# Turning eight gated heads on VectorE and through DRAM instead of on TensorE, in a one-core hybrid mixer block

## The chip, the cores and the metric

The kernel runs on 1 core of one Trainium2 chip. The metric is the device time of one execution in microseconds (us). Three runs of the kernel before gave 973.75 us as the median, 973.37 and 974.31 us as the ends.

## What is computed

One layer of a streaming encoder on 512 positions with 1024 channels. The input is normalised, projected once, and the columns are split among three mixers and three merge gates; the merged result is projected, a SwiGLU sub-layer and a gated per-layer embedding follow. The change touches the first mixer and its gate:

```python
hn = rms_norm(h, g_mix_pre)
proj = hn @ w_in
z_sgu, z_conv, z_pool, z_gate = jnp.split(proj, SPLITS, axis=-1)
u, v = jnp.split(gelu(z_sgu), 2, axis=-1)
v = layer_norm(v, g_v, b_v)
# 8 heads of 128 channels, 4 blocks of 128 positions
mixed = einsum('hij,bnjhc->bnihc', w_masked, v) + b_s        # mixes positions inside a block
br_a = (u * mixed) @ w_sgu_out
# causal depthwise convolution, width 31, then layer norm and silu: branch b
merged = gates[0] * br_a + gates[1] * br_b + gates[2] * br_c
```

## The kernel before, in words

The kernel works on the transpose: channels stand on the 128 partitions, the 512 positions along the free axis. Each matrix product is done three times in a reduced-width float type (`mm3`): high half times high half, high times low, low times high. So each 128x1024 block of weights is read from DRAM into a buffer `raw` (3 of them, queue of SyncE), copied to `hi` by ScalarE and subtracted to `lo` by VectorE (3 buffers each); a tile of 128 output channels is 24 matmuls with 512 columns. `Weights.get` takes the next block and starts loading so that two more are ahead. The load of a block waits for the `lo` of the block three before it; its `hi` waits until TensorE has left the `hi` of three tiles before.

The spatial gating unit needs the positions on the partitions. So `natural` computes `v` and then `u` with positions on the partitions: for each of two halves of 512 channels four weight blocks (`kk`), and for each the four position blocks, two position blocks before the yield with `behind` 0 and two after it. `mix_head(h)` splits the head's `v` into halves (`v_split`), multiplies it with the head's 128x128 position matrix (3 matmuls into `ps_mix`), and VectorE computes `gated = (ps_mix + b) * u`, 128 positions by 4 blocks of 128 channels. `turn_head(h)` brings the channels back to the partitions: four TensorE transposes of 128x128 into `ps_tr`, then a ScalarE copy (high) and a VectorE subtraction (low) into `sgu_T[h]`.

The heads are mixed and turned between other products: heads 0 to 3 are mixed during the last four weight blocks of `u` (dictionary `heads`), heads 4 to 7 after the gate tiles 0 to 2; heads 0 and 1 are turned during `u`, 2 to 7 after gate tiles 0 to 3. `SGU_LAG` is the number of gate tiles that come before the first branch tile: `for n in range(KT + SGU_LAG)` makes gate tile n (24 matmuls, `ps_gate`, sigmoid by ScalarE into `merged[:, n]`) and, from `n = SGU_LAG` on, branch tile `n - SGU_LAG` (24 matmuls over the eight `sgu_T`, `ps_br`), which VectorE multiplies into `merged`. Branch tile 0 takes the heads in order, so head 7 is needed last, by matmuls 22 to 24.

VectorE works off the depthwise convolution in the background: 8 groups of channels, for each one start instruction and 30 taps (`conv_tap`, `acc <- h_conv, vec, acc`), each tap reading what the one before wrote. `drain(n)` takes the next n entries of the list `background`; `TAPS = (4, 3, 5, 3, 5)` says how many after each product: `TAPS[2]` in the gate and branch tiles of the gating unit, `TAPS[3]` in the `z` tiles of the pooling branch, `TAPS[4]` in the pooling branch's gate and branch tiles. What is left is drained before the last of these; then the sum over the channels of the convolution goes to TensorE (`ps_stat`) for the layer norm.

The order of the instructions on each engine is made when the kernel is built, by a list scheduler with a timeline of its own: among the instructions that it holds for ready, the one written first in the program goes first. `order()` pins VectorE, ScalarE and TensorE instructions written inside it behind what was written before them on their engine; taps and `gated` are so pinned, the halves `lo`, `v_split` and `sgu` are not. DMAs go through the queue of SyncE (SP) in the order that the scheduler gives.

Of the kernel before, what the change touches and what calls it, by code (L numbers as in the profile page):

```python
# [7 lines left out]

F32 = mybir.dt.float32
F32R = mybir.dt.float32r  # L10
# [2 lines left out]
AF = mybir.ActivationFunctionType  # L13
ALU = mybir.AluOpType
PSUM = bass.MemoryType.PSUM

P = 128
T = 512
H = 256
D = 1024  # L20
KT = D // P
NB = T // P
WIDTH = 31
DFF = 2816
FT = DFF // P
# [17 lines left out]

N_WARM = 8

TAPS = (4, 3, 5, 3, 5)
TAPS_U = 4


# [42 lines left out]
def hybrid_block(  # L92
# [7 lines left out]
    nc = tc.nc  # L100
    order = InOrder(tc)
    dve, act_e = order.engine(nc.vector), order.engine(nc.scalar)
    pe_order = InOrder(tc)
    pe = pe_order.engine(order.engine(nc.tensor))

    const = ctx.enter_context(tc.tile_pool(name="const", bufs=1))
    stream = ctx.enter_context(tc.tile_pool(name="stream", bufs=3))
    wide = ctx.enter_context(tc.tile_pool(name="wide", bufs=2))
# [5 lines left out]
    def bank(name):  # L114
        return psum.tile([P, T], F32, tag="ps", name=name)

    def wide_tile(name):
        return wide.tile([P, KT, T], F32, tag="wide", name=name)

    def slot(tag, name, dt=F32R, shape=(2, T)):  # L120
        return act.tile([P, *shape], dt, tag=tag, name=name, bufs=6 if tag == "tm" else 8)

    def t2(name, n=T):
        return tmp.tile([P, n], F32, tag="t2", name=name)
# [4 lines left out]

    vec = const.tile([P, N_VEC + WIDTH * KT], F32, name="vec")  # L130
    x_all = wide_tile("x_all")
# [19 lines left out]
    def col(name, k):  # L151
        i = VECS.index(name) * KT + k
        return vec[:, i:i + 1]

    def tap(k, j):
        i = N_VEC + k * WIDTH + j
        return vec[:, i:i + 1]
# [7 lines left out]
    ps = psum.tile([P, T], F32, tag="pst", name="ps_warm", bufs=1)  # L165
    for n in N_WARM * (T,) + (H,):
        pe.matmul(ps[:, :n], lhsT=warm_up[:, :P], rhs=warm_up[:, :n], start=True, stop=True)
    ident = const.tile([P, P], F32, name="ident")
    make_identity(nc, ident)
    cnt_i = const.tile([P, WINDOWS[-1]], I32, name="cnt_i")  # L170
    nc.gpsimd.iota(cnt_i, pattern=[[1, WINDOWS[-1]]], base=1, channel_multiplier=0)
    rcnt = const.tile([P, WINDOWS[-1]], F32, name="rcnt")
# [4 lines left out]
    def split(hi, lo, src):  # L177
        act_e.copy(hi, src)
        dve.tensor_tensor(out=lo, in0=src, in1=hi, op=ALU.subtract)
# [142 lines left out]
    def add_mix(*blocks):  # L322
        for b in blocks:
            weights.add(w_mix[b])
# [3 lines left out]
    add_mix(*range(C_V, C_V + 8))  # L328
    weights.add(w_sgu, "tm")
    add_mix(*range(C_U, C_U + 8))  # L330
    SGU_LAG = 4
    for n in range(KT + SGU_LAG):
        if n < KT:
            add_mix(C_M + n)
        if n >= SGU_LAG:
            add_mix(S_SGU + n - SGU_LAG)
    for g in GROUPS:
# [121 lines left out]
    with order():  # L459
        (c0, c1), cut = first_cuts(0)  # L460
        hi, lo = (w[:, c0:c1] for w in first[0])
# [4 lines left out]
        hi, lo = (w[:, slice(*cut)] for w in first[0])  # L466
# [55 lines left out]
    for k in range(N_RAW, KT):  # L522
        pair = []
        for _ in range(2):
            ps = bank("ps_ag")
# [3 lines left out]
            pair.append(ps)  # L529
            drain(TAPS[0])  # L530
        glu(k, *pair)


    def natural(dst, evacuate, taps):


        for c in range(2):
            banks = [bank("ps_nat") for _ in range(NB)]
            for kk in range(4):
                hi, lo = weights.get()  # L540
                for b in range(NB):
                    if b == NB // 2:
                        yield c, kk, 0
# [12 lines left out]
                if kk == 3:  # L556
                    for b in range(NB):
                        evacuate(dst, b, c, banks[b])
                yield c, kk, 1

    def blocks_of(t):
        return t.rearrange("p a b -> p (a b)").rearrange("p (n c) -> p n c", n=NB)

    v_all = blocks_of(wide_tile("v_all"))
    v_stats = const.tile([P, NB, 2, 6], F32, name="v_stats")

    def v_gelu(dst, b, c, ps):
        cs = slice(c * T, (c + 1) * T)
        act_e.activation(out=dst[:, b, cs], in_=ps, func=AF.Gelu_apprx_tanh)
        dve.bn_stats(out=v_stats[:, b, c, :], in_=dst[:, b, cs])  # L570

    g_bc = slot("tm", "g_bc", F32, (D,))
    nc.sync.dma_start(out=g_bc, in_=gb_v[0:1, :].broadcast_to([P, D]))
    b_bc = slot("tm", "b_bc", F32, (D,))
    nc.sync.dma_start(out=b_bc, in_=gb_v[1:2, :].broadcast_to([P, D]))
    for _ in natural(v_all, v_gelu, TAPS[1]):
        pass
# [11 lines left out]
                                scalar2=v_y[:, b:b + 1], op0=ALU.subtract, op1=ALU.mult)  # L589

    def v_gain(b):
        dve.tensor_tensor(out=v_all[:, b], in0=v_all[:, b], in1=g_bc, op=ALU.mult)
        nc.gpsimd.tensor_tensor(out=v_all[:, b], in0=v_all[:, b], in1=b_bc, op=ALU.add)

    background[:0] = [lambda f=f, b=b: f(b) for b in range(NB) for f in (v_norm, v_gain)]

# [1 line left out]
    for w in (sg_hi, sg_lo):  # L598
        masked = w.rearrange("p (h i) -> p h i", h=KT)
        dve.memset(masked[64:128, :, 0:64].bitcast(F32), 0.0)  # L600
    u_all = blocks_of(wide_tile("u_all"))

    def u_gelu(dst, b, c, ps):
        act_e.activation(out=dst[:, b, c * T:(c + 1) * T], in_=ps, func=AF.Gelu_apprx_tanh)

    sgu_T = [None] * KT
    gated = [None] * KT

    def mix_head(h):
        cs = slice(h * P, (h + 1) * P)  # L610
        vs = slot("tm", "v_split", shape=(2, NB, P))
        split(vs[:, 0], vs[:, 1], v_all[:, :, cs])
        ps = bank("ps_mix")
        mm3(ps, sg_hi[:, cs], sg_lo[:, cs], vs[:, 0], vs[:, 1], True, True)
        gated[h] = t2("gated")
        with order():
            dve.scalar_tensor_tensor(
                out=gated[h].rearrange("p (n c) -> p n c", n=NB),
                in0=ps.rearrange("p (n c) -> p n c", n=NB),
                scalar=col("b_sgu_s", h), in1=u_all[:, :, cs], op0=ALU.add, op1=ALU.mult)  # L620

    def turn_head(h):
        pt = bank("ps_tr")
        for b in range(NB):
            bs = slice(b * P, (b + 1) * P)
            pe.transpose(out=pt[:, bs], in_=gated[h][:, bs], identity=ident)
        sgu_T[h] = slot("br", f"sgu{h}")
        split(sgu_T[h][:, 0], sgu_T[h][:, 1], pt)


    heads = {(1, 0): ((), (0,)), (1, 1): ((), (1,)), (2, 1): ((0,), (2,)),
             (3, 0): ((1,), ()), (3, 1): ((), (3,))}
    for c, kk, behind in natural(u_all, u_gelu, 0):
        pe_order.on = c == 1 or kk == 3
        turned, mixed = heads.get((kk, behind), ((), ())) if c == 1 else ((), ())
        for h in turned:
            turn_head(h)
        for h in mixed:
            mix_head(h)
        if behind:  # L640
            drain(TAPS_U)
# [3 lines left out]
    merged = wide_tile("merged")  # L645
# [17 lines left out]

    for n in range(KT + SGU_LAG):
        if n < KT:
            gate_tile(merged[:, n, :], TAPS[2])
        if n < SGU_LAG:
            for h in ((2,), (3, 4), (5,), (6, 7))[n]:
                turn_head(h)
            for h in ((4,), (5, 6), (7,), ())[n]:  # L670
                mix_head(h)
        else:
            i = n - SGU_LAG
            ps = branch_tile(sgu_T, TAPS[2])
            dve.tensor_tensor(out=merged[:, i, :], in0=ps, in1=merged[:, i, :], op=ALU.mult)


    z_all = wide_tile("z_all")
# [86 lines left out]
    for n in range(KT):  # L765
        ps = branch_tile(conv_T, 0)
        t = t2("br")
# [66 lines left out]
    with order():  # L834
# [6 lines left out]
        for i in range(N_HALF):  # L841
            n = KT - N_HALF + i
# [9 lines left out]
        for i in range(N_HALF):  # L852
            n = KT - N_HALF + i
# [79 lines left out]
    for n in range(KT - 2):  # L933
        ps = bank("ps_fo")
# [31 lines left out]
    with order():  # L966
        ps, ps_last = bank("ps_fo"), bank("ps_fo")
# [40 lines left out]
        for n in range(N_LAST, KT - 1):  # L1008
            ps = bank("ps_pg")
# [24 lines left out]
def _arrays(x, p, g_mix_pre, w_in, w_sgu_s, b_sgu_s, g_sgu_v, b_sgu_v, w_sgu_out, w_dw, b_dw,  # L1034
# [51 lines left out]
```

## Time and profile before

| | |
|---|---|
| median of three runs | 973.75 us |
| the profiled execution's own time | 974.28 us |
| its span, first to last instruction | 972.5 us |
| TensorE (PE) busy | 966.9 us, 99% |
| VectorE (DVE) busy | 673.3 us, 69% |
| ScalarE (ACT) busy | 349.9 us, 36% |
| GpSimd (POOL) busy | 70.9 us, 7% |
| granted TensorE clock | 1.0 |
| bytes read from HBM and written to it | 97.68 MB, 2.10 MB |

The profile is of one execution, 0.53 us above the median. The share of busy time is a mean over stages with different limits; the views that matter are the chain of work that ended last, the engines' busy time by stretch, and the timeline around the gating unit, from about 155 to 278 us of the span.

### The profile page before, as it was taken

The numbers are of one execution on the slowest core, as the hardware profiler recorded it, in microseconds if no ns is written. First come the engines' busy times: TensorE is split into PE (matmuls) and PEld (weight loads), VectorE is DVE, ScalarE is ACT, GpSimd is POOL, SyncE is SP. The second block draws the span as 40 slices with busy tenths as digits, with TensorE's granted clock in tenths as the row PEclk, the third lists the DMA queues.
The fourth block names the chain that finished last, engine by engine and source line by source line (L and its number), as shares of the span: only waits on it lengthen the run. The fifth ranks groups of instructions, "written<-read, shape, count | busy, mean of one in ns | idle before, by whom it ended". The sixth has DMA issues, their size and how long they took to land.

```text
span 972.5 us, 11143 instructions
## 1 busy us (share of the span) xinstructions
PE 966.9 (99%) x4429; PEld 804.4 (83%) x4429; DVE 673.3 (69%) x868; ACT 349.9 (36%) x467; POOL 70.9 (7%) x51
## 2 busy tenths in 40 slices
PE   9999999999999999999999999999999999999998
PEld 6888888888888888888888988888888888888887
DVE  6997789999988899987555787544444442223684
ACT  7622333432224432156425353323232322223451
POOL 0100004000013712130000000000000000000000
PEclk9999999999999999999999999999999999999999
DMA  8832331322322332232337203222322333334311
GB/s 291 197 109 87 110 107 66 108 87 87 109 85 78 98 108 87 94 123 87 109 97 263 74 26 105 87 97 98 99 97 89 104 82 99 99 100 144 109 66 65
DMA packets 30724, 102.72 MB, mean 106 GB/s; under 512 B 3536, under 2 KB 4048, under 8 KB 30672
## 3 DMA queue, kind: packets, MB, share of 16 engines
q1 hardware_dynamic: 29808, 99.75, 31.0%
q0 software_dynamic: 720, 2.23, 1.3%
q8 instruction: 34, 0.56, 0.2%
q14 instruction: 18, 0.15, 0.0%
q10 hardware_dynamic: 144, 0.04, 0.0%
HBM read 97.68 MB, written 2.10 MB: 103 GB/s over the span
## 4 chain that ended last, share of the span: by engine, by line
PE 99%; DMA 1%; SPq 0%; DVE 0%; ACT 0%; issue 0%; DVEq 0%
PE ps_f L79 25%; PE ps_gate L79 13%; PE ps_br L79 13%; PE ps_fo L79 12%; PE ps_nat L79 9%; PE ps_ag L79 6%; PE ps_o L79 5%; PE ps_pg L79 5%; PE ps_z L79 4%; PE ps_first L79 3%; PE ps_ple L79 1%; PE ps_pool L79 1%; DMA first_all<-in_w_first 1%; PE ps_mix L79 1%; PE ps_stat L79 0%; PE ps_tr L79 0%
## 5 line engine op out<-in xcount | busy, mean ns | idle before, releaser
L79 ACT CAST hi<-raw 128x1024 fp32r<-128x1024 f32 (+2 forms) x160 | 165.2, 1033 | 459.4 <-PE ps_br L79 82.5
L79 DVE TENSOR_TENSOR lo<-raw,hi 128x1024 fp32r<-128x1024 f32 (+2 forms) x158 | 206.9, 1310 | 110.0 <-ACT hi L79 109.7
L79 DVE SCALAR_TENSOR_TENSOR acc<-h_conv,vec,acc 128x511 f32<-128x511 f32 (+14 forms) x240 | 183.1, 763 | 5.0
L79 PE MATMUL ps_f<-hg,hi 128*128 128x512 f32 (+1 forms) x608 | 183.3, 383 | 0.0
L79 PEld LDWEIGHTS ps_f<-hg,hi 128*128 128x128 f32 x608 | 113.1, 188 | 22.4
L79 PE MATMUL ps_gate<-hn,hi 128*128 128x512 f32 x384 | 119.0, 389 | 0.0
L79 PE MATMUL ps_f<-hg,lo 128*128 128x512 f32 (+1 forms) x304 | 116.4, 383 | 0.0
L79 PE MATMUL ps_fo<-f,hi 128*128 128x512 f32 x352 | 108.3, 389 | 0.0
L79 PEld LDWEIGHTS ps_gate<-hn,hi 128*128 128x128 f32 x384 | 72.0, 188 | 15.1
L79 PE MATMUL ps_nat<-hi,hn 128*128 128x512 f32 x256 | 78.8, 389 | 0.0
L79 PEld LDWEIGHTS ps_fo<-f,hi 128*128 128x128 f32 x352 | 66.1, 188 | 13.7
L79 PE MATMUL ps_gate<-hn,lo 128*128 128x512 f32 x192 | 74.8, 389 | 0.0
L79 PE MATMUL ps_fo<-f,lo 128*128 128x512 f32 x176 | 68.5, 389 | 0.0
L79 PEld LDWEIGHTS ps_f<-hg,lo 128*128 128x128 f32 x304 | 57.1, 188 | 11.3
L79 DVE TENSOR_TENSOR f<-ps_f,h_inv 128x512 f32<-128x512 f32 x22 | 15.2, 690 | 59.3 <-PE ps_f L79 59.3
L79 PEld LDWEIGHTS ps_nat<-hi,hn 128*128 128x128 f32 x256 | 48.0, 188 | 9.9
L79 PE MATMUL ps_nat<-lo,hn 128*128 128x512 f32 x128 | 49.8, 389 | 0.0
L79 PE MATMUL ps_ag<-hn,hi 128*128 128x512 f32 x160 | 49.2, 389 | 0.0
L79 PEld LDWEIGHTS ps_gate<-hn,lo 128*128 128x128 f32 x192 | 36.0, 188 | 7.5
L79 DVE TENSOR_TENSOR silu<-ps_f,h_inv 128x512 f32<-128x512 f32 x22 | 15.2, 690 | 36.7 <-PE ps_f L79 36.6
L79 PE MATMUL ps_br<-pool,hi 128*128 128x512 f32 x128 | 39.6, 389 | 0.0
L79 PE MATMUL ps_br<-sgu,hi 128*128 128x512 f32 x128 | 39.4, 389 | 0.0
(223 smaller groups left out, 1490.6 us busy)
## 6 DMA issues: line engine op xcount, KB each, us to landing
raw<-in_w_mix SPq DMA_DIRECT2D x90, 512.0 KB, 3.2
raw<-in_w_ffn_in SPq DMA_DIRECT2D x44, 512.0 KB, 3.2
raw<-in_w_ffn_out SPq DMA_DIRECT2D x16, 448.0 KB, 3.3
raw<-in_w_ffn_out SPq DMA_DIRECT2D x8, 512.0 KB, 3.5
raw<-in_w_ple_gate SPq DMA_DIRECT2D x8, 512.0 KB, 3.9
x_all<-in_xT SPq DMA_DIRECT2D x8, 256.0 KB, 7.2
h_all<-in_xT SPq DMA_DIRECT2D x4, 512.0 KB, 5.4
out_dram<-pg SPq DMA_DIRECT2D x7, 256.0 KB, 2.0
```

The costliest lines, as they stand in the source:

```text
L79: inst = op(*args, **kw)
```

## The change

The gated head is no longer transposed by TensorE. VectorE transposes it in blocks of 32 by 32 (`dve.transpose`, right behind `gated`, both pinned). What then still has to move, whole blocks of 32 partitions, goes through DRAM: four writes of 32 partitions each (pieces of 128 elements, 512 bytes) into a DRAM tile `home` (8 of them), and one read of 128x512 back into the low half of `sgu_T[h]`. `split_head(h)` copies it to the high half (ScalarE) and subtracts (VectorE), now from SBUF instead of PSUM. So that a block of 32 columns is a block of 32 channels, `v` and `u` lie head by head, within a head by groups of 32 channels and then by position block; the positions of `sgu_T` and of the branch tiles stand in another order, and the multiplication into `merged` puts them back by its access pattern. The identity matrix goes. `SGU_LAG` is 5: branch tile 0 comes after gate tile 5, where it came after gate tile 4, and the heads are split after gate tiles 0 to 4. `TAPS[3]` is 4: one tap more after each of the 8 `z` tiles.

```diff
-TAPS = (4, 3, 5, 3, 5)
+TAPS = (4, 3, 5, 4, 5)
...
+    dram = ctx.enter_context(tc.tile_pool(name="dram", bufs=KT, space=bass.MemoryType.DRAM))
...
-    ident = const.tile([P, P], F32, name="ident")
-    make_identity(nc, ident)
...
-    SGU_LAG = 4
+    SGU_LAG = 5
...
     def blocks_of(t):
-        return t.rearrange("p a b -> p (a b)").rearrange("p (n c) -> p n c", n=NB)
+        return t.rearrange("p a b -> p (a b)").rearrange("p (g n a) -> p n g a", n=NB, a=Q)
+    def of_head(t, h):
+        return t[:, h]
+    def grouped(t):
+        return t.rearrange("p (g a) -> p g a", a=Q)
...
-        split(vs[:, 0], vs[:, 1], v_all[:, :, cs])
+        split(vs[:, 0], vs[:, 1], of_head(v_tile, h))
...
+        gated, corners = t2("gated"), t2("corners")
+        sgu_T[h] = slot("br", f"sgu{h}")
         with order():
+            dve.scalar_tensor_tensor(out=gated, in0=ps, scalar=col("b_sgu_s", h),
+                                     in1=of_head(u_tile, h), op0=ALU.add, op1=ALU.mult)
+            dve.transpose(out=corners, in_=gated)
+        home = dram.tile([P, T], F32, name="home")
+        for i in range(NQ):
+            nc.sync.dma_start(
+                out=home[:, i * P:(i + 1) * P].rearrange("(q a) f -> a q f", q=NQ),
+                in_=corners[i * Q:(i + 1) * Q].rearrange("a (q f) -> a q f", q=NQ))
+        nc.sync.dma_start(out=sgu_T[h][:, 1].bitcast(F32), in_=home)
 
-    def turn_head(h):
-        pt = bank("ps_tr")
-        for b in range(NB):
-            bs = slice(b * P, (b + 1) * P)
-            pe.transpose(out=pt[:, bs], in_=gated[h][:, bs], identity=ident)
-        sgu_T[h] = slot("br", f"sgu{h}")
-        split(sgu_T[h][:, 0], sgu_T[h][:, 1], pt)
+    def split_head(h):
+        hi, lo = sgu_T[h][:, 0], sgu_T[h][:, 1]
+        split(hi, lo, lo.bitcast(F32))
...
-            for h in ((2,), (3, 4), (5,), (6, 7))[n]:
-                turn_head(h)
-            for h in ((4,), (5, 6), (7,), ())[n]:
+            for h in ((2,), (3,), (4,), (5, 6), (7,))[n]:
+                split_head(h)
+            for h in ((4,), (5, 6), (7,), (), ())[n]:
                 mix_head(h)
...
-            dve.tensor_tensor(out=merged[:, i, :], in0=ps, in1=merged[:, i, :], op=ALU.mult)
+            gate = merged[:, i, :].rearrange("p (n i b) -> p i n b", n=NB, i=NQ)
+            dve.tensor_tensor(out=gate, in0=ps.rearrange("p (i n b) -> p i n b", n=NB, i=NQ),
+                              in1=gate, op=ALU.mult)
```

More of the change, by code (lines that the diff above doesn't have):

```diff
@@ L6 @@
 from concourse._compat import with_exitstack
-from concourse.masks import make_identity
 F32 = mybir.dt.float32
@@ L22 @@
 NB = T // P
+Q = 32
+NQ = P // Q
 WIDTH = 31
@@ L561, in blocks_of @@
     def blocks_of(t):
-        return t.rearrange("p a b -> p (a b)").rearrange("p (n c) -> p n c", n=NB)
-    v_all = blocks_of(wide_tile("v_all"))
+        return t.rearrange("p a b -> p (a b)").rearrange("p (g n a) -> p n g a", n=NB, a=Q)
[3 more added lines that the diff above has]
+        return t.rearrange("p (g a) -> p g a", a=Q)
+    v_tile = wide_tile("v_all")
+    v_all = blocks_of(v_tile)
     v_stats = const.tile([P, NB, 2, 6], F32, name="v_stats")
     def v_gelu(dst, b, c, ps):
-        cs = slice(c * T, (c + 1) * T)
-        act_e.activation(out=dst[:, b, cs], in_=ps, func=AF.Gelu_apprx_tanh)
-        dve.bn_stats(out=v_stats[:, b, c, :], in_=dst[:, b, cs])
+        v = dst[:, b, c * T // Q:(c + 1) * T // Q]
+        act_e.activation(out=v, in_=grouped(ps), func=AF.Gelu_apprx_tanh)
+        dve.bn_stats(out=v_stats[:, b, c, :], in_=v)
     g_bc = slot("tm", "g_bc", F32, (D,))
@@ L591, in v_gain @@
     def v_gain(b):
-        dve.tensor_tensor(out=v_all[:, b], in0=v_all[:, b], in1=g_bc, op=ALU.mult)
-        nc.gpsimd.tensor_tensor(out=v_all[:, b], in0=v_all[:, b], in1=b_bc, op=ALU.add)
+        dve.tensor_tensor(out=v_all[:, b], in0=v_all[:, b], in1=grouped(g_bc), op=ALU.mult)
+        nc.gpsimd.tensor_tensor(out=v_all[:, b], in0=v_all[:, b], in1=grouped(b_bc), op=ALU.add)
     background[:0] = [lambda f=f, b=b: f(b) for b in range(NB) for f in (v_norm, v_gain)]
@@ L600, in hybrid_block @@
         dve.memset(masked[64:128, :, 0:64].bitcast(F32), 0.0)
-    u_all = blocks_of(wide_tile("u_all"))
+    u_tile = wide_tile("u_all")
+    u_all = blocks_of(u_tile)
     def u_gelu(dst, b, c, ps):
-        act_e.activation(out=dst[:, b, c * T:(c + 1) * T], in_=ps, func=AF.Gelu_apprx_tanh)
+        act_e.activation(out=dst[:, b, c * T // Q:(c + 1) * T // Q], in_=grouped(ps),
+                         func=AF.Gelu_apprx_tanh)
     sgu_T = [None] * KT
-    gated = [None] * KT
     def mix_head(h):
         cs = slice(h * P, (h + 1) * P)
-        vs = slot("tm", "v_split", shape=(2, NB, P))
-        split(vs[:, 0], vs[:, 1], v_all[:, :, cs])
+        vs = slot("tm", "v_split")
+        split(vs[:, 0], vs[:, 1], of_head(v_tile, h))
         ps = bank("ps_mix")
         mm3(ps, sg_hi[:, cs], sg_lo[:, cs], vs[:, 0], vs[:, 1], True, True)
-        gated[h] = t2("gated")
+        gated, corners = t2("gated"), t2("corners")
+        sgu_T[h] = slot("br", f"sgu{h}")
         with order():
[L617 to L620, printed above, removed]
-    def turn_head(h):
-        pt = bank("ps_tr")
-        for b in range(NB):
-            bs = slice(b * P, (b + 1) * P)
-            pe.transpose(out=pt[:, bs], in_=gated[h][:, bs], identity=ident)
-        sgu_T[h] = slot("br", f"sgu{h}")
-        split(sgu_T[h][:, 0], sgu_T[h][:, 1], pt)
+            dve.scalar_tensor_tensor(out=gated, in0=ps, scalar=col("b_sgu_s", h),
[10 more added lines that the diff above has]
+        split(hi, lo, lo.bitcast(F32))
     heads = {(1, 0): ((), (0,)), (1, 1): ((), (1,)), (2, 1): ((0,), (2,)),
@@ L634, in hybrid_block @@
         pe_order.on = c == 1 or kk == 3
-        turned, mixed = heads.get((kk, behind), ((), ())) if c == 1 else ((), ())
-        for h in turned:
-            turn_head(h)
+        done, mixed = heads.get((kk, behind), ((), ())) if c == 1 else ((), ())
+        for h in done:
+            split_head(h)
         for h in mixed:
@@ L667, in hybrid_block @@
         if n < SGU_LAG:
-            for h in ((2,), (3, 4), (5,), (6, 7))[n]:
-                turn_head(h)
-            for h in ((4,), (5, 6), (7,), ())[n]:
+            for h in ((2,), (3,), (4,), (5, 6), (7,))[n]:
+                split_head(h)
+            for h in ((4,), (5, 6), (7,), (), ())[n]:
                 mix_head(h)
```

## The prediction

> **What bounds the kernel now.** I read the page first: the span, the busy shares, the chain.
>
> ```profile
> span 972.5 us, 11143 instructions
> PE 966.9 (99%) x4429; PEld 804.4 (83%) x4429; DVE 673.3 (69%) x868; ACT 349.9 (36%) x467; POOL 70.9 (7%) x51
> PEclk9999999999999999999999999999999999999999
> PE 99%; DMA 1%; SPq 0%; DVE 0%; ACT 0%; issue 0%; DVEq 0%
> ```
>
> TensorE is busy for 966.9 of 972.5 us at full granted clock and is 99% of the chain. No wait can be taken away: the time falls only by work that leaves TensorE, and rises by every wait that is put into it. Next, how close the other engines are, by three stretches: the gating unit, the `z` tiles, the pooling branch up to the convolution's sum.
>
> ```profile
> core 0: us, PE busy (x) PEld busy (x) DVE busy (x) ACT busy (x) POOL busy (x), PEclk, DMA share, GB/s
> 138.00:277.00 139.00, 139.00 (x630) 115.25 (x629) 135.88 (x174) 43.27 (x58) 16.25 (x7) 1.00 0.26 88
> 277.00:337.00 60.00, 60.00 (x266) 49.67 (x266) 49.18 (x57) 23.46 (x31) 24.82 (x18) 1.00 0.27 86
> 337.00:421.00 84.00, 84.00 (x372) 69.53 (x371) 82.65 (x96) 22.76 (x27) 21.29 (x14) 1.00 0.32 106
> ```
>
> The reader is to see that VectorE, 69% on average, is full where the heads are turned (135.88 of 139) and again from 337 us; only the `z` tiles leave it 10.8 us. ScalarE and the DMA engines have room everywhere.
>
> **What goes: 32 transposes.** The chain in order of time around them, with the shares by line of its window of 70 us (155 to 225):
>
> ```profile
> by line: PE ps_gate L79 41.6%; PE ps_nat L79 38.0%; PE ps_mix L79 7.9%; PE ps_br L79 7.8%; PE ps_tr L79 5.0%
> 168.53 2.72 PE ps_nat L79 x12
> 171.25 0.68 PE ps_mix L79 x3
> 177.38 0.44 PE ps_tr L79 x4
> 177.81 0.70 PE ps_mix L79 x3
> 178.52 2.75 PE ps_nat L79 x12
> 205.31 0.70 PE ps_mix L79 x3
> 211.49 0.87 PE ps_tr L79 x8
> 217.83 5.44 PE ps_br L79 x24
> 228.71 5.44 PE ps_br L79 x24
> ```
>
> The transposes are 5.0% of 70 us, 3.5 us (0.109 us each, 0.44 us a head). Behind them the next pieces are longer than the same pieces elsewhere: 0.70 against 0.68 for three matmuls, 2.75 against 2.72 for twelve, 0.05 us at each of six places, 0.25 us in all. TensorE gets back **3.75 us**; the identity was made off the chain and is worth nothing. The Trainium skill, "VectorE: DVE Perf Modes", section "The three transpose paths", gives 390 ns for a TensorE transpose of 128x128 (bf16); by that 32 of them would be 12.5 us and the time about 961.5 us. The trace differs: the chain has 3.5 us of them, so I give that outcome no chance.
>
> **What comes: VectorE.** The nearest rows by size are the other operations on 128x512:
>
> ```profile
> L79 DVE SCALAR_TENSOR_TENSOR gated<-ps_mix,vec,u_all x8: 741/744/746, 175.1 to 209.7; 128x512 f32<-128x512 f32 x8
> L79 DVE TENSOR_TENSOR sgu<-ps_tr,sgu x8: 677/682/689, 184.0 to 217.0; 128x512 fp32r<-128x512 f32 x8
> L79 ACT CAST sgu<-ps_tr x8: 576/582/601, 178.1 to 213.2; 128x512 fp32r<-128x512 f32 x8
> L79 DVE TENSOR_TENSOR v_split<-v_all,v_split x8: 678/682/689, 164.8 to 190.3; 128x512 fp32r<-128x512 f32 x8
> L79 ACT CAST v_split<-v_all x8: 607/620/625, 162.5 to 185.7; 128x512 fp32r<-128x512 f32 x8
> L79 DVE TENSOR_SCALAR acc<-h_conv,vec x4: 542/543/2196, 200.5 to 340.1; 128x512 f32<-128x512 f32 x4
> L79 DVE TENSOR_TENSOR lo<-raw,hi x25: 691/1219/2319, 163.0 to 297.3; 128x1024 fp32r<-128x1024 f32 x24, 128x512 fp32r<-128x512 f32 x1
> ```
>
> No block transpose stands in the trace. Its lower end is the one-input 0.54 us, its upper end the twice as large `lo` with 1.22 us (each element costing double); I take 0.70 us, between the 0.68 and 0.74 us of the same size. Eight are 5.6 us (4.3 to 9.8). The splits change source only: VectorE takes 0.682 us from PSUM (`sgu`) and from SBUF (`v_split`), ScalarE 0.58 and 0.62 us, so 0.3 us more on ScalarE, which is idle half of the time. The new layouts of `v`, `u` and `merged` keep every count of elements; runs of 32 I price at nothing, the cover being ScalarE's idle time, and on VectorE each 0.1 us on their 20-odd instructions would be 2 us of the same lag as the transposes'.
>
> **What comes: the way through DRAM,** eight times four writes and a read on the SP queue.
>
> ```profile
> L205 SPq DMA_DIRECT2D raw<-in_w_mix x23: 327/328/328, 164.2 to 298.5; - x23
> raw<-in_w_mix SPq DMA_DIRECT2D x90, 512.0 KB, 3.2
> out_dram<-pg SPq DMA_DIRECT2D x7, 256.0 KB, 2.0
> raw<-in_w_pool SPq DMA_DIRECT2D x4, 256.0 KB, 2.6
> SPq L205 <- DVE lo L79: 121.5, 24, 7.8
> ACT hi L79 <- PE ps_gate L79: 34.0, 8, 5.2
> ```
>
> One issue is 0.33 us, so a head is 1.6 us of SP's time and 13 us in all. A write of 64 KB I take at the 2.0 us of the store of 256 KB, the read at the 2.6 us of the load of the same 256 KB; a quicker trip gains nothing, since nothing waits for it then; the upper end is 3.2 us and an issue of 0.33 us more on each, if a 512 KB weight load goes ahead of it in the queue. Behind the waiting writes stand the weight loads. SP sits idle for 121.5 us from 160 to 290 until a buffer is free, and the `hi` casts then wait 34.0 us in 8 cases for TensorE to leave a buffer, none for a load: a load 4 us late is covered, and the wait for a head's writes (2 us plus 1.6 us of issue) is within that.
>
> **Where it can reach TensorE: head 7 in branch tile 0.** VectorE's timeline, kernel before:
>
> ```profile
> 190.28 0.69 DVE L79 TENSOR_TENSOR v_split<-v_all,v_split 128x512 fp32r<-128x512 f32 x1
> 209.74 0.75 DVE L79 SCALAR_TENSOR_TENSOR gated<-ps_mix,vec,u_all 128x512 f32<-128x512 f32 x1
> 211.66 3.08 DVE L79 SCALAR_TENSOR_TENSOR acc<-h_conv,vec,acc 128x506 f32<-128x506 f32 x4
> 216.44 1.28 DVE L79 TENSOR_TENSOR sgu<-ps_tr,sgu 128x512 fp32r<-128x512 f32 x2
> 220.61 1.22 DVE L79 TENSOR_TENSOR lo<-raw,hi 128x1024 fp32r<-128x1024 f32 x1
> ```
>
> `gated` of head 7 starts at 209.74, on an engine without idle time; seven transposes ahead of it make that 214.6, its end 215.4, its transpose's end 216.1. The fourth write is issued 1.0 us later and lands 2.0 us on, 219.1; the read lands at 221.7; ScalarE 222.3; VectorE finishes a tap (up to 0.77, 3.08 over 4) and subtracts (0.68): 223.0 to 223.8. Needed: branch tile 0 began at 217.83, now 5.44 later for the gate tile put ahead and 3.75 earlier, 219.5; head 7 comes 21 of 24 matmuls in, 224.3. That is 0.5 to 1.3 us in hand. The cover is that gate tile; without it all is 5.4 us late. Since the margin is smaller than the doubt on the round trip I charge **0.3 us** of wait (ends 0 and 2.6 us, one transfer behind a load, 3.5, less the middle of the margin, 0.9).
>
> **What is late next: the taps.** VectorE has 5.6 us more to do and TensorE passes 3.4 us sooner, so the taps fall 9.0 us behind. The small halves need not: at 190.28 the half of head 7's `v` went in between taps, long before its use after 205. The taps' reckoning comes at the convolution's sum:
>
> ```profile
> DVE lo L79 <- ACT hi L79: 5.4, 5, 2.0
> DVE pool L79 <- ACT pool L79: 3.3, 2, 2.9
> 418.36 1.78 DVE L79 TENSOR_TENSOR sum_half<-conv_sum,sum_half 128x512 fp32r<-128x512 f32 x1
> 420.79 0.39 PE L79 MATMUL ps_stat<-sum_half,mean_mat 128*128 128x512 f32 x1
> ```
>
> The sum is ready at 420.14 and TensorE takes it at 420.79, 0.65 us in hand. Ahead of it, in the `z` stretch, VectorE has 10.8 us without work, most of it waits that a late tap can fill (5.4 us for `hi`, 3.3 us for `pool`). `TAPS[3]` moves 8 taps, 6.2 us at 0.77, from the pooling branch to the `z` tiles: 9.0 and 6.2 less 10.8 leaves 4.4 us behind at 337, and the 6.2 us that are then missing turn that into 1.8 us ahead. I cost it at nothing; the `z` stretch is its cover.
>
> **The sum,** against the profiled execution: 974.28 - 3.75 + 0.3 = 970.8 us. That execution is 0.53 us above the median of the runs, so 970.3 us, 0.35% less. A measurement of this kernel tells about 0.2% (1.9 us) from no change.
>
> **The rivals.**
> 1. VectorE becomes the bound in the gating unit. If taps keep their place ahead of the weights' `lo`, the one that ended at 221.83 ends 5.6 us later, 227.4. Its tile began at 228.71, the matmul that takes it 0.45 later (two of 0.227), and all that 3.75 sooner is 225.4. TensorE waits 2.0 us: 972.5 us, 972.0 against the median. With 1.22 us a transpose the `lo` ends 9.8 us later, the wait is 6.2 us and the time 976.2 us. For it: 135.88 of 139. Against: the row at 190.28. Chance 0.25, nine tenths of it up to 975.0.
> 2. The round trip is slow, and the change is slower. Place: head 7 in branch tile 0. If the last write and the read each go behind a weight load, the trip is 7.1 us longer, TensorE waits 6.2 us (0.9 in hand), and the time is 974.28 - 3.75 + 6.2 less 0.53: 976.2 us. The trip of 4.6 us may grow by 0.9 before it costs anything, by 4.6 before the gain is gone, by 6.6 before it is measurably slower. For it: a weight load goes through the same queue in every tile. Against: the scheduler may let TensorE go on with gate tile 6. Chance 0.18. A harsher form is that short pieces slow the write: 512 bytes each, where the stores in the trace have whole rows. The same section of the Trainium skill warns that a plain DMA whose access pattern makes the transposition is 19 times slower than one through the transposing unit; by that the write would take 38 us and the time be near 1005 us. No run here shows such pieces; they are contiguous, and VectorE has done the transposition within them: chance 0.02.
> 3. The taps are not made up. If only half of the 10.8 us can be filled, 9.0 - 5.4 - 0.65 = 2.95 us of waiting at `ps_stat`: 973.0 us against the median, no change. Against: the waits in the `z` tiles are for `hi` and `pool`, which a tap can precede. Chance 0.08.
>
> **How the numbers follow.** The forecast has 0.47; its own range is 969.7 (no wait, and the spread of the runs) to 971.3 us (1.3 us of wait). Faster by over 0.2% is below 971.8 us: 0.47 and 0.08 of rival 1 (waits under 1.8 us), 0.55. No change: 0.14 of rival 1 and rival 3, 0.22. Slower: rival 2 with its harsher form, 0.20, and 0.03 of rival 1, 0.23. The range of 969.7 to 975.0 leaves out rival 2 and the worst of rival 1.
>
> **What would show it.** Right: no `ps_tr`; gate and branch tiles follow each other with matmuls every 0.227 us from 185 on; a block transpose of 0.6 to 0.8 us behind each `gated`; writes landing in about 2 us and reads in under 3; head 7's subtraction done before the 22nd matmul of branch tile 0; VectorE with less than 5 us idle from 277 to 337. Wrong: a gap on TensorE in branch tile 0 released by `sgu` (rival 2), by `lo` in several tiles (rival 1), or at `ps_stat` (rival 3); a transpose of 1.2 us; ScalarE waiting for a read while `hi` casts stand behind it.

## The result, and the profile after

The change made the kernel slower: 981.62 us as the median of four runs (979.13 to 982.34) against 974.0 us for the kernel before, a ratio of 1.0077 with an interval of 1.0064 to 1.0089. The forecast was 970.3 us. The profiled execution took 981.05 us. Of the experiments below, one run of e13 took 1631 us and one of the kernel before, beside e14, 1073 us, at granted clocks of 0.56 and 0.85; the times and ratios leave these two out. From the page of the profiled execution, the span, the busy shares, the granted clock and the chain that ended last:

```profile
span 979.1 us, 11157 instructions
PE 967.0 (99%) x4397; PEld 803.4 (82%) x4397; DVE 679.1 (69%) x876; ACT 349.0 (36%) x467; POOL 70.8 (7%) x49
PEclk9999999999998999999999999999999999999999
PE 79%; DVE 15%; issue 3%; DMA 2%; ACT 0%; SPq 0%; DVEq 0%; ACTq 0%
```

TensorE has 32 instructions fewer, and its busy time is still 967 us: some of its matmuls ran slower. The chain, 99% TensorE before, has left it for VectorE in 15% of the span, and one slice of forty shows a clock below full. By stretch of the kernel (the gating unit, the `z` tiles, the pooling branch; the columns are busy time and count of each engine, the granted clock and the share of the DMA engines):

```profile
138.00:273.00 135.00, 134.63 (x594) 111.19 (x593) 127.66 (x168) 41.89 (x57) 14.43 (x6) 1.00 0.38 119
273.00:333.00 60.00, 54.48 (x225) 44.15 (x224) 56.46 (x68) 18.49 (x25) 20.87 (x14) 0.94 0.26 85
333.00:425.00 92.00, 90.77 (x401) 74.58 (x400) 86.90 (x96) 26.39 (x32) 28.08 (x17) 1.00 0.29 98
```

The gating unit, where the change was made, lost almost nothing: TensorE is busy for 134.63 of 135 us. The loss is in the `z` tiles behind it, where TensorE stood for 5.5 of 60 us and ran at a mean clock of 0.94. What TensorE waited for from 150 to 430 us, and what VectorE waited for from 160 to 290 us (total, times, longest, in us):

```profile
PE ps_pool L80 <- ACT pl_hi L80: 5.5, 2, 3.1
PE ps_gate L80 <- DVE lo L80: 1.2, 1, 1.2
PE ps_br L80 <- DVE lo L80: 0.4, 1, 0.4
```

```profile
DVE sgu L80 <- ACT sgu L80: 5.9, 4, 2.2
```

The two waits are at the pool maps, the small products `ps_pool` over the moving windows that are made between the `z` tiles. VectorE, on the other hand, stood for 5.9 us in the gating unit before it could subtract a head.

**The first wait.** The timeline of VectorE, with TensorE's and GpSimd's rows at the same place:

```profile
287.55 1.18 POOL L705 COPY win<-z_all 128x2 f32<-128x2 f32 x1
288.60 3.07 DVE L80 SCALAR_TENSOR_TENSOR acc<-h_conv,vec,acc 128x505 f32<-128x505 f32 x4
292.19 2.28 DVE L80 SCALAR_TENSOR_TENSOR acc<-h_conv,vec,acc 128x501 f32<-128x501 f32 x3
294.39 1.21 DVE L80 SCALAR_TENSOR_TENSOR win<-win,z_all 128x1020 f32<-128x1020 f32 x1
297.58 0.73 PE L80 MATMUL ps_pool<-pl_hi,hi 128*128 128x512 f32 x2 [2.42 <-ACT pl_hi L80]
```

GpSimd's part of the window ended at 288.73. VectorE took its own part at 294.39, 5.66 us later, because seven taps and a `lo` stood ahead of it in VectorE's queue. Before, the same distance was 1.4 us (292.04 to 293.45). TensorE's last matmul ahead of the map began at 294.77 and the next could have begun 0.227 us later, so TensorE lost 2.58 us; the view's 2.42 counts from the modelled end of that matmul.

**The second wait,** on VectorE after and, in the second fence, before:

```profile
304.75 0.63 POOL L705 COPY win<-win 128x4 f32<-128x4 f32 x1
311.88 1.20 DVE L80 SCALAR_TENSOR_TENSOR win<-win,z_all 128x1016 f32<-128x1016 f32 x1
313.01 0.15 DVE L80 TENSOR_TENSOR win<-win,rcnt 128x8 f32<-128x8 f32 x1
313.08 0.71 DVE L80 SCALAR_TENSOR_TENSOR acc<-h_conv,vec,acc 128x487 f32<-128x487 f32 x1
313.72 1.21 DVE L80 TENSOR_TENSOR lo<-raw,hi 128x1024 fp32r<-128x1024 f32 x1
314.86 0.15 DVE L80 TENSOR_TENSOR win<-win,z_all 128x8 f32<-128x8 f32 x1
```

```profile
306.43 0.63 POOL L689 COPY win<-win 128x4 f32<-128x4 f32 x1
307.69 1.21 DVE L79 SCALAR_TENSOR_TENSOR win<-win,z_all 128x1016 f32<-128x1016 f32 x1
308.82 0.16 DVE L79 TENSOR_TENSOR win<-win,rcnt 128x8 f32<-128x8 f32 x1
309.01 0.17 DVE L79 TENSOR_TENSOR win<-win,z_all 128x8 f32<-128x8 f32 x1
```

Before, VectorE's three steps of the window begin 0.63 us behind GpSimd's part and follow each other. After, VectorE comes to the first step 6.50 us behind GpSimd's part (305.38 to 311.88), with taps, two `lo` and two `pool` ahead of it, and a tap and a `lo` stand between the second step and the third, 1.78 us. ScalarE's `pl_hi` and TensorE's map can only come behind the third; TensorE lost 3.26 us.

**The clock behind the waits.** The busy times of the 3.5 us from 299.0 on, a little after the first wait:

```profile
299.00:302.50 3.50, 3.50 (x11) 2.69 (x10) 3.46 (x3) 0.00 (x0) 3.38 (x3) 0.51 0.48 150
```

The granted clock is 0.51, and the matmuls follow each other every 0.427 us instead of 0.227. The clock record holds half speed for 3.4 us at 299.1 and again at 316.1. The Trainium skill, "TensorE: Matmul & The Clock Gate", "Why this matters for your kernels", advises against pauses of over about 3 us between bursts of matmuls, since one idle window brings the clock down to half. The trace is stricter: here 2.58 us were enough.

**The account,** by adding up what the distances between TensorE's matmuls exceed 0.227 us: first pool map 2.69 us and 1.59 us at half clock; second 3.63 and 1.50; branch tile 0, 0.64; a gate tile at 345.5, 1.50; another spot 0.11. That is 11.66 us put in. Taken out: 3.75 us of transposes, and 1.19 us in the first 13 us of the span, where TensorE starts on the input and the change does nothing (this part differs from run to run). The net is 6.7 us; the spans differ by 6.6 us.

### The profile page after: what moved, and what is told of

Read it like the earlier page. It is cut to its first block, busy times and chain, and to the rows that moved or that the text cites. A ratio compares the mean times of both kernels' runs of the same rounds, so it can differ in the third digit from the quotient of the medians.

```text
span 979.1 us, 11157 instructions
## 1 busy us (share of the span) xinstructions
PE 967.0 (99%) x4397; PEld 803.4 (82%) x4397; DVE 679.1 (69%) x876; ACT 349.0 (36%) x467; POOL 70.8 (7%) x49
## 4 chain that ended last, share of the span: by engine, by line
PE 79%; DVE 15%; issue 3%; DMA 2%; ACT 0%; SPq 0%; DVEq 0%; ACTq 0%
PE ps_f L80 25%; PE ps_fo L80 12%; PE ps_br L80 9%; PE ps_gate L80 8%; DVE acc L80 8%; PE ps_ag L80 6%; PE ps_o L80 5%; PE ps_pg L80 4%; PE ps_nat L80 4%; DVE lo L80 4%; PE ps_first L80 3%; PE ps_ple L80 1%; DMA sgu<-home 1%; DVE v_all L80 1%; DMA home<-corners 1%
## 5 line engine op out<-in xcount | busy, mean ns | idle before, releaser
L80 DVE SCALAR_TENSOR_TENSOR acc<-h_conv,vec,acc 128x509 f32<-128x509 f32 (+14 forms) x240 | 188.5, 790 | 4.3
L80 PE MATMUL ps_z<-hn,hi 128*128 128x512 f32 x128 | 41.6, 406 | 0.0
```

The lines of the kernel that those rows point to most:

```text
L80: inst = op(*args, **kw)
```

## The experiments

Three theories of where the time comes from. The first: the 8 taps moved by `TAPS[3]` overfill VectorE in the `z` tiles. The second: the way through DRAM makes VectorE, which works its queue in order, stand before a split, and what is late there is paid in the `z` tiles. The third: the 5.6 us of block transposes alone do it. All can hold in part, so each was taken out alone and with others. Each kernel was timed beside the kernel before on the same chip; ratios are against that. The kernel before gave 973.6 to 974.0 us in these comparisons, so a difference between the times of two experiments carries a doubt of some 0.4 us from that alone.

**e1_taps3: the change without the moved taps**

```diff
-TAPS = (4, 3, 5, 4, 5)
+TAPS = (4, 3, 5, 3, 5)
```

> The changed kernel with TAPS[3] back at 3, so 8 taps (6 us of VectorE) leave the z tiles. In the changed kernel TensorE waits 2.6 and 3.3 us at two pool maps in the z tiles, and its clock is halved for 3.4 us after each. Theory A (VectorE has too much work: eight transposes of 0.70 us and 8 taps more ahead of the pool windows): the second wait shrinks by most of 4 us and the first by about 2, so both waits and one or both of the slow stretches go, 972 to 975 us. Theory B (VectorE lost 5.9 us standing at head 7 and others for the way through DRAM, and stays late): those 5.9 us are still lost before the z tiles, the waits shrink by 1 to 3 us, 976 to 979 us. Theory C (the taps alone): 970.5 us.

976.41 us, ratio 1.0025 (1.0015 to 1.0036). Of the 7.6 us, 5.2 go. TensorE's and VectorE's main waits:

```profile
PE ps_pool L80 <- ACT pl_hi L80: 2.6, 2, 2.4
DVE sgu L80 <- ACT sgu L80: 6.8, 4, 2.5
```

The first pool map still waits, with half clock for 3.4 us behind it, and VectorE's standing before the heads is there in full. The taps are the larger part and not all. Two more waits, at branch tile 0, are for a `lo` (0.8 us) and, this time, for a `hi` of ScalarE (0.3 us).

**e2_before_taps4: the moved taps alone, in the kernel before**

```diff
-TAPS = (4, 3, 5, 3, 5)
+TAPS = (4, 3, 5, 4, 5)
```

> The kernel before with TAPS[3] = 4 alone. Theory C (the taps alone make the waits at the pool maps): 978 to 982 us. Theories A and B (the z tiles have 10.8 us free on VectorE in the kernel before, so 6.2 us fit): 974 us, no change within 1.5 us.

975.04 us, ratio 1.0015 (1.0005 to 1.0024). TensorE's only wait behind the loading of the input is in a gate tile of the pooling branch, none is at a pool map:

```profile
PE ps_gate L79 <- DVE lo L79: 1.3, 1, 1.3
```

The same 8 taps cost 1.5 us here (975.04 against 973.59 us for the kernel before in this comparison) and 5.2 us in the changed kernel. They cost little by themselves; they cost more where VectorE comes late into the `z` tiles, or where its queue is woven otherwise.

**e3_no_dram: the change without the way through DRAM.** The split reads the block-transposed head directly, without writes and read.

```diff
-        home = dram.tile([P, T], F32, name="home")
-        for i in range(NQ):
-            nc.sync.dma_start(out=home[...], in_=corners[...])
-        nc.sync.dma_start(out=sgu_T[h][:, 1].bitcast(F32), in_=home)
+        turned[h] = corners
...
-        split(hi, lo, lo.bitcast(F32))
+        split(hi, lo, turned[h])
```

> The changed kernel without the way through DRAM: the split reads what VectorE transposed (32 by 32 blocks are left in the wrong places, so the output is not the reference's); no write, no read, everything else the same. Theory B (VectorE's 5.9 us of standing still for the reads): VectorE has no such wait, is up to 5.9 us earlier at the pool maps, and the time is 970 to 974 us. Theory A (work): VectorE is as late at the z tiles as its work makes it, 977 to 981 us.

974.35 us, ratio 1.0007 (0.9998 to 1.0016); against the change, 7.3 us less. The waits of TensorE and of VectorE:

```profile
PE ps_pool L80 <- ACT pl_hi L80: 2.8, 1, 2.8
DVE sgu L80 <- ACT sgu L80: 0.7, 1, 0.7
```

VectorE stands before the heads for 0.7 us instead of 5.9. One pool map, the second, still waits, with 6.8 us of half clock behind it. That execution is the slowest of ten, with 976.21 us. The mean granted clock of the ten goes with their times: 1.0 in the four of 972.77 to 973.54 us, 0.998 in four from 974.26 to 975.88 us, 0.996 in two (975.95 us and the profiled one). So the half clock doesn't come in every execution of the same kernel, and it makes up to 3 us of difference. The DMA way has a large part in the loss although no wait of TensorE names it.

**e4_before_turn: the block transposes alone, in the kernel before**

```diff
+            dve.transpose(out=t2("corners"), in_=gated[h])
```

Its result isn't used; the heads are turned by TensorE as before.

> The kernel before, TensorE transposing, with a block transpose of each gated head on VectorE besides, whose result nobody reads: 5.6 us of VectorE's work and nothing else of the change. Theory A: VectorE is 5.6 us later at the z tiles, the first pool map has about 2 us in hand and the second 1, so TensorE waits 2 to 4 us there and loses a slow stretch or two: 977 to 980 us. Theory B: the free time in the z tiles takes it, 974 to 975 us.

974.34 us, ratio 1.0007 (0.9997 to 1.0016): no change. The one wait is of 0.4 us:

```profile
PE ps_mix L79 <- DVE gated L79: 0.4, 1, 0.4
```

So 5.6 us more on a VectorE that is busy for 135.88 of 139 us cost nothing measurable in the kernel before: its taps move on (157 are begun when the `z` tiles begin, where it was 161), into time that is free later. The third theory, taken alone, falls.

**e7_no_dram_taps3: both taken away** (e3 with `TAPS[3]` at 3)

```diff
-TAPS = (4, 3, 5, 4, 5)
+TAPS = (4, 3, 5, 3, 5)
```

> The changed kernel with both: no way through DRAM (the split reads the blocks where VectorE left them, so the output is not the reference's) and TAPS[3] = 3. Theory AB (VectorE's lateness is a sum of its waits for the reads, the taps moved and the transposes, and TensorE stalls only beyond 2 to 3 us of it): no wait of TensorE at the pool maps, no slow clock, the 3.75 us of the transposes come back whole: 969.5 to 970.5 us. Theory D (the layouts or the shorter TensorE path alone make it late): a wait and a slow stretch stay, 973 us or more.

970.77 us, ratio 0.9970 (0.9959 to 0.9981). No pool map waits; what is left is the wait that the third rival spoke of:

```profile
PE ps_stat L80 <- DVE sum_half L80: 0.6, 1, 0.6
```

With three taps per `z` tile, the way through DRAM costs 976.41 - 970.77 = 5.6 us; with four, 7.3 us.

**e10_no_turn: e3 without the block transposes as well,** four taps. The split reads the gated head itself.

```diff
-        gated, corners = t2("gated"), t2("corners")
+        gated = t2("gated")
...
-            dve.transpose(out=corners, in_=gated)
-        turned[h] = corners
+        turned[h] = gated
```

> e3_no_dram (TAPS[3] = 4, no DRAM) also without VectorE's block transposes: the split reads the gated head as it is (output not the reference's). 5.6 us less of VectorE's work. Theory A (the transposes' 5.6 us take part in the lateness): the 3.0 us wait of e3_no_dram at the second pool map goes, 970 to 971 us. If the 8 taps moved are enough alone beside a TensorE that is 3.75 us earlier: the wait stays, 973 to 975 us.

971.61 us, ratio 0.9978 (0.9969 to 0.9987). TensorE's wait is that of e2, and no pool map waits:

```profile
PE ps_gate L80 <- DVE lo L80: 1.2, 1, 1.2
```

The transposes, worth nothing in e4, are worth 2.7 us here (974.35 - 971.61), beside the fourth tap; against the four runs of e3 with full clock (973.41 us in the middle) it is 1.8 us. The loads on VectorE don't simply add up: the transposes alone (e4, e7) or the moved taps alone (e2, e10) make no pool map late; transposes with taps (e3) or with standing before the heads (e1) do, and then the clock can drop.

**e8_late: the way through DRAM kept, the splits put behind their data.** Three taps; no split during `u`; the splits one gate tile later (head 6 two) and pinned, on ScalarE as on VectorE, behind what is written ahead of them; branch tile 0 after gate tile 6. These were changed together, and which of them does it was not separated.

```diff
-TAPS = (4, 3, 5, 4, 5)
+TAPS = (4, 3, 5, 3, 5)
...
-    SGU_LAG = 5
+    SGU_LAG = 6
...
-        split(hi, lo, lo.bitcast(F32))
+        with order():
+            split(hi, lo, lo.bitcast(F32))
...
-    heads = {(1, 0): ((), (0,)), (1, 1): ((), (1,)), (2, 1): ((0,), (2,)),
-             (3, 0): ((1,), ()), (3, 1): ((), (3,))}
+    heads = {(1, 0): ((), (0,)), (1, 1): ((), (1,)), (2, 1): ((), (2,)),
+             (3, 1): ((), (3,))}
...
-            for h in ((2,), (3,), (4,), (5, 6), (7,))[n]:
+            for h in ((0, 1), (2,), (3,), (4,), (5,), (6, 7))[n]:
```

> The changed kernel with the way through DRAM, TAPS[3] = 3, and the splits later and pinned in program order: heads 0 and 1 after gate tile 0, 2 to 5 after gate tiles 1 to 4, 6 and 7 after gate tile 5, branch tile 0 after gate tile 6 (SGU_LAG = 6). The work is that of e1_taps3. Theory B (the place of the subtraction in VectorE's queue, ahead of its data, is what costs): VectorE waits under 1.5 us for the reads instead of 6.8, TensorE does not wait at the pool maps: 969.5 to 971.5 us. Theory A (work): as e1_taps3, 975 to 977 us.

971.78 us (971.63 to 972.54), ratio 0.9981 (0.9972 to 0.9990), 4.6 us less than e1. VectorE's wait for heads is gone, and its busy time in the gating unit is 132.94 of 135 us, where the change has 127.66; ScalarE, too, waits for no read any more; one short wait at the second pool map is left, without half clock:

```profile
138.00:273.00 135.00, 135.00 (x597) 111.81 (x597) 132.94 (x173) 42.74 (x58) 14.82 (x6) 1.00 0.39 123
```

```profile
PE ps_pool L80 <- ACT pl_hi L80: 1.6, 1, 1.6
```

Beside e7 the way through DRAM now costs 1.0 us where it cost 5.6. So most of its price hung on where the splits stand, in the queues and among the tiles, not on the transfer.

**e9_late_taps4: e8 with the moved taps**

```diff
-TAPS = (4, 3, 5, 3, 5)
+TAPS = (4, 3, 5, 4, 5)
```

> e8_late with TAPS[3] = 4 as in the change. Theory B with the additive lateness: as e3_no_dram, one wait of about 3 us at the second pool map with a slow stretch, 973 to 975 us. If the waits for the reads were all: 970 to 971 us.

980.68 us, ratio 1.0071 (1.0057 to 1.0085): 8.9 us for 8 taps of 0.73 us, and more than 5 us above both expected times, so lateness doesn't simply add up either. VectorE doesn't stand for heads, so that part of the second theory isn't needed for the loss. Two pool maps wait, and VectorE is full in the stretch (58.95 of 60 us); the waits of TensorE, VectorE's and GpSimd's timeline, and the busy times of the `z` tiles and of the time behind the second wait:

```profile
PE ps_pool L80 <- ACT pl_hi L80: 7.6, 2, 5.2
```

```profile
312.73 2.92 DVE L80 TENSOR_TENSOR lo<-raw,hi 128x1024 fp32r<-128x1024 f32 x1
329.91 1.85 DVE L80 TENSOR_TENSOR win<-win,rcnt 128x16 f32<-128x16 f32 x1
329.00 2.73 POOL L705 TENSOR_TENSOR win<-win 128x1020 f32<-128x1020 f32 x1
```

```profile
273.00:333.00 60.00, 54.81 (x241) 44.75 (x239) 58.95 (x63) 18.53 (x25) 27.45 (x19) 1.00 0.24 79
334.20:341.00 6.80, 5.62 (x13) 4.51 (x14) 6.76 (x6) 2.49 (x3) 3.17 (x3) 0.50 0.17 40
```

VectorE's instructions are also longer where GpSimd works on its windows: a `lo` takes 2.92 us instead of 1.22, and the 128x16 product, 0.16 us in e8, takes 1.85 us and ends at 331.76, just behind the GpSimd row that starts at 329.00 and ends at 331.73. The Trainium skill, "GPSIMD Engine Reference", "8. Key points", says that GpSimd shares its SBUF interfaces with VectorE and that VectorE's instructions in a two-port mode or with two SBUF inputs contend with it; these rows, of two inputs each, agree. A `lo` of 2.92 us stands in e8 too (at 311.93), so this alone isn't the loss of e9. By the distance between matmuls the two waits are 2.51 and 5.38 us; behind the second follow 6.8 us at clock 0.50.

**e11_taps5_2: e8 with the taps where VectorE has time.** Five after each tile of an earlier stretch (45 to 98 us), two in the `z` tiles.

```diff
-TAPS = (4, 3, 5, 3, 5)
+TAPS = (5, 3, 5, 2, 5)
```

> e8_late (splits later and pinned, SGU_LAG = 6) with TAPS = (5, 3, 5, 2, 5): 10 taps, 7.7 us of VectorE's work, go into the ag tiles from 50 to 100 us, where VectorE has 9 us free in e8_late, and 8 taps leave the z tiles. Theory of the sum (what counts is how late VectorE is at the pool maps): the 1.75 us wait of e8_late at the second pool map goes, 969.5 to 970.3 us, 0.4% under the kernel before. If the wait stays, the pool maps are held by something else than VectorE's load (GpSimd's windows, the scheduler's order): 971.5 to 972 us.

**970.64 us** (970.06 to 970.9), ratio **0.9966** (0.9954 to 0.9979): the best of all, and better than both kernels. In the gating unit and the `z` tiles:

```profile
138.00:273.00 135.00, 135.00 (x597) 111.80 (x596) 132.99 (x172) 43.06 (x58) 16.82 (x7) 1.00 0.38 121
273.00:333.00 60.00, 60.00 (x266) 49.68 (x265) 46.17 (x57) 22.26 (x30) 25.83 (x20) 1.00 0.30 96
```

TensorE has no wait from 150 to 430 us, and VectorE has 13.8 us of the 60 free. The span is 4.3 us shorter than before: the 3.75 us of the transposes, and 0.52 us in the first 13 us.

**e12_before_taps5_2 and e13_after_taps5_2: the same taps in the kernel before and in the change**

```diff
-TAPS = (4, 3, 5, 3, 5)          # e12, the kernel before
-TAPS = (4, 3, 5, 4, 5)          # e13, the change
+TAPS = (5, 3, 5, 2, 5)
```

> The kernel before with TAPS = (5, 3, 5, 2, 5) alone. TensorE has no wait to lose there, so no change: 973 to 974.5 us. If the moved taps are worth time by themselves, e11_taps5_2 owes its gain to them and not to the transposes that left TensorE: under 972 us.

> The changed kernel itself, splits and SGU_LAG = 5 as in the change, with TAPS = (5, 3, 5, 2, 5): VectorE is about 14 us less late at the pool maps than in the change (8 taps there, 8 against e1 by half, and 10 taps done early), although it still stands for the reads. Theory of the sum: no wait at the pool maps, only what is left at branch tile 0 (0.6 to 1.5 us): 970.5 to 972 us. If VectorE's waits for the reads cost by themselves and not through lateness: 974 us or more.

e12: 974.06 us, ratio 1.0004 (0.9995 to 1.0012), no change, so e11 doesn't gain by its taps alone; the turn itself, at equal taps, is worth 974.06 - 970.64 = 3.4 us. e13: 975.38 us, ratio 1.0019 (1.0010 to 1.0028). The waits of e13:

```profile
PE ps_pool L80 <- ACT pl_hi L80: 1.8, 1, 1.8
PE ps_gate L80 <- DVE lo L80: 1.7, 2, 1.3
DVE sgu L80 <- ACT sgu L80: 6.2, 5, 2.2
```

With its taps out of the way the change as written still loses 4.7 us to e11, about what e1 loses to e8 (4.6): the place of the splits, with the one gate tile more, is a loss of its own, and VectorE's 6.2 us of standing come back as waits for `lo` and at the first pool map.

**e14_taps5_4: early like e11, but four taps in the `z` tiles.** This separates two readings of e9: that VectorE comes too late into the stretch, or that taps stand between the steps of a window. In e14 VectorE has begun 163 taps when the `z` tiles begin, as in e11 (153 in e8 and e9).

```diff
-TAPS = (5, 3, 5, 2, 5)
+TAPS = (5, 3, 5, 4, 5)
```

> e9_late_taps4 with TAPS[0] = 5: 10 taps are done before the gating unit, VectorE comes to the z tiles 10 taps (7.7 us) further, but 4 taps still follow each z tile. In e9_late_taps4 TensorE waits 2.5 and 5.4 us at two pool maps. Theory L (how late VectorE comes to the z tiles decides): both waits go, 970.5 to 972 us. Theory P (the taps put between the pool windows decide, where VectorE's instructions stretch from 1.2 to 2.9 us beside GpSimd's): a wait of 3 us or more stays at the second or third pool map, 975 us or more.

975.48 us, ratio 1.0020 (1.0010 to 1.0029), 4.8 us more than e11:

```profile
PE ps_pool L80 <- ACT pl_hi L80: 3.8, 1, 3.8
```

Not lateness alone: with VectorE as early as in e11, the fill of the `z` tiles still makes the second pool map late; half clock for 3.4 us follows. Being early helps (e9 lost twice as much) and doesn't cure.

## Why the prediction was wrong

- **The gain on TensorE: right.** No `ps_tr` is left, and where nothing else was disturbed (e11) the span shows all of the 3.75 us; that e11's 970.64 us is 0.3 us from what was forecast for the change says that this term was sized right, not that the forecast of the change held.
- **VectorE's price: right in size.** The block transpose, estimated at 0.70 us, and the path of the heads:

```profile
L80 DVE STREAM_TRANSPOSE corners<-gated x8: 700/702/709, 175.1 to 212.7; 128x512 f32<-128x512 f32 x8
L80 DVE TENSOR_TENSOR sgu<-sgu x8: 680/692/1162, 182.4 to 221.8; 128x512 fp32r<-128x512 f32 x8
L634 SPq DMA_DIRECT2D home<-corners x32: 303/432/1186, 175.9 to 215.7; - x32
DMA to landing us min/median/max: 1.6/2.6/3.6
```

  0.702 us, and the subtraction at 0.692 us, its source making no difference. The taps fell 11 behind (161 begun when the `z` tiles began, now 150): at 0.77 us that is 8.5 us, where 9.0 were forecast. That the two agree is luck: without the way through DRAM (e3, 154 begun; e7, 155) it is 6 or 7 taps, about 5 us, and the rest comes with VectorE's standing, which the forecast doesn't have.
- **The round trip: too short, without effect where it was looked for, at head 7.** A write took 2.6 us in the median, not 2.0, and from the end of the transpose to the landing of the read a head took 5.9 to 7.8 us instead of 5.6. Head 7 took 7.7 us, but its transpose began at 212.73 instead of 215.4; its subtraction was over at 222.54, and TensorE needed it at about 223.6. The second rival (a slow trip stops branch tile 0) didn't occur, in its harsher form neither: short pieces landed in at most 3.6 us.
- **Branch tile 0: 0.64 us of wait, forecast 0.3, for another reason.** It is at the third matmul, released by a `lo` and not by a head. It isn't the first rival either, since e3 and e7 have the transposes and no such wait. The `hi` of this `lo` ended on ScalarE only at 217.54, behind two splits for which ScalarE had stood 5.01 and 3.04 us until their reads landed, and the `lo` itself (217.89 to 219.11) came behind a split for which VectorE had stood 1.43 us.
- **The step that failed: "I cost it at nothing; the `z` stretch is its cover."** The 10.8 us that VectorE has free there before were counted as time in which late taps can go. e1 prices the moved taps at 5.2 us in the change, e9 at 8.9, e14 against e11 (16 taps) at 4.8. The free time lay between steps of a chain (GpSimd's window, VectorE's part, `pl_hi`, the pool map) that must be ready when TensorE comes; a tap put there delays the map, and the work that was bound for `ps_stat`, some 100 us later, was called in at 295 and 313 us. With four taps the cover came true only where VectorE had no block transposes to do: in e2 and e10 no pool map waits. The third rival had the right cause in the wrong place, and at 2.95 us less than a third of the 9.4 us that the two maps cost.
- **The term that was missing: the wait of VectorE and ScalarE for the reads.** The prediction asked whether a read makes TensorE wait, named ScalarE waiting for a read with `hi` casts behind it as a sign of being wrong, and gave VectorE no wait. The sign came:

```profile
ACT sgu L80 <- DMA sgu<-home: 33.3, 8, 10.3
```

  ScalarE stood before all eight reads, mostly in time in which it had stood for TensorE's gate tiles before (34.0 us, now 8.4). VectorE stood for 5.9 us, before heads whose split was in its queue ahead of their data; putting the splits behind it on both engines, with one gate tile more, gave back 4.6 us (e1 to e8) and 4.7 us (e13 to e11). Which of the two engines' standing costs more was not separated. That "nothing waits for it then" was true of TensorE, which never waited for a head itself, and false of the engine whose taps are the reserve.
- **The clock: not priced.** 3.1 of the 9.4 us at the pool maps are matmuls at half speed behind the wait.

Left open is why four taps per `z` tile spare the pool maps in the kernel before (e2) and in e10, and not in the changed kernel or e14. The runs show that the order on VectorE's queue differs (a tap and a `lo` between two steps of a window), and that GpSimd's windows lengthen VectorE's instructions; that the scheduler's own timeline sets this order differently when the DMA way is in the program is argued, not shown.

## What to carry to other kernels

Work taken off the bounding engine is gained only if the engine that receives it has time near that place, and its idle time isn't the slack of a chain that the bounding engine waits for: look for each idle stretch's next consumer before filling it. An instruction that needs a DMA's result, in an in-order queue, belongs behind the landing (here one gate tile later, with branch tile 0 later too, 4.6 and 4.7 us), even where the bounding engine isn't waiting for it. Background work goes where the receiving engine is free for long. The two together turned a loss of 7.6 us into a gain of 3.1 (e11).

## What was not expected of the hardware

- In these traces the clock of TensorE fell to half after waits as short as 2.53 us, and not after every one: taken as the distance between two matmuls beyond 0.227 us, after 2.58 and 3.26 us (the change), 2.53 us (e1) and 4.0 us (e14) it fell for 3.4 us, after 3.0 us (e3) and 5.4 us (e9) for 6.8 us; after 2.51 us (e9) and all shorter ones (1.4 us in e2 and e10, 1.75 in e8, 1.99 in e13) it didn't. Of e3's ten runs four show full clock throughout; their waits were not traced.
- VectorE's instructions beside GpSimd's windows grew: in e9 a `lo` from 1.22 to 2.92 us, a tap from 0.73 to 2.38 us (at 326.49), the 128x16 product from 0.16 to 1.85 us. The `lo` of 312.73 ended at 315.65, 1.08 us behind the GpSimd instruction of 312.29 to 314.57, and the tap at 328.87, 0.55 us behind the one of 326.14 to 328.32, as if they had stood until it was done; that they did is read from these times and was not tested.
- Writes of 64 KB in pieces of 512 bytes landed after 1.6 us at the least and 3.6 us at the most, with weight loads in the same queue.
